# Forming every third low part of a mixer's later weights on GpSimd instead of VectorE

## The chip, the cores and the metric

The kernel runs on one core of a Trainium2 chip. The metric is the device time in microseconds, as the median of several runs. Five engines of the core matter here: PE (TensorE, the matrix products), DVE (VectorE), ACT (ScalarE), POOL (GpSimd) and SP (SyncE, which here only issues DMA transfers). Each engine works through its own instructions strictly in the order in which the program gives them, and waits on semaphores for the others.

## The reference

Two layers over 256 tokens of width 1024, all in float32. Cut to what matters:

```
for l in range(2):
    h = h + 0.5 * swiglu(rms_norm(h, ffn1_norm[l]), ffn1_w_in[l], ffn1_w_out[l])
    u = rms_norm(h, mix_norm[l])
    z_s, xbc, dt_s, qkv, z_d, b_d, a_d, gate_s, gate_d = split(u @ w_in[l])
    y_s = mamba2_branch(z_s, xbc, dt_s, ...)      # SSD in chunks of 128: decay matrices, a gated norm
    y_d = deltanet_branch(qkv, z_d, b_d, a_d, ...)  # gated delta rule in chunks of 64, a gated norm
    merged = sigmoid(gate_s) * (y_s @ ssm_w_branch[l]) + sigmoid(gate_d) * (y_d @ dn_w_branch[l])
    h = h + merged @ w_out[l]
    h = h + 0.5 * swiglu(rms_norm(h, ffn2_norm[l]), ffn2_w_in[l], ffn2_w_out[l])
return rms_norm(h, final_norm)
```

## The kernel before

All weights are streamed from DRAM once, as half units of 128 x 1024 float32. For each, SP issues a DMA into one of five buffers (`wraw`). ACT makes a copy rounded to a shorter float form (`whi`, the high part, line 68), and DVE subtracts: `wlo = wraw - whi` (the low part, line 71). PE then forms three products for each piece of weights, high by high, high by low and low by high, which together stand for a float32 product. `whi` and `wlo` have five buffers each, so parts are made some units ahead of PE, and a weight buffer comes free when its low part is done. The function `prep(i)` makes the two parts of half unit i of the list `plan`; `take()` hands PE the next one and starts loads and parts ahead.

Each layer is a feed-forward part, the mixer and a second feed-forward part. In the mixer, the string `ORDER` is the sequence of steps in the program: `z`, `k`, `q`, `v`, `b`, `d`, `x`, `g` with digits are steps that take two half units each (projections of the input), and `N` takes eight (the product of the delta branch with its output weights). Other letters are steps without weights: `s` scalars, `M` masks, `I` the triangular inverse, `R` the recurrence, `P` the products of the SSD branch with themselves, `D` the decay matrices, `S` and `T` the SSD products of one of four groups, `o` and `y` the first transposes for the two output products.

Names that the later parts use, with lines of the profile:

- `xs` (lines 340, 345, 346): PE's projection to a group's SSD input; `ca` (line 74): its short convolution, three steps on DVE per tile; `xsT`: the result, made by ACT; `xsb` (line 1101): PE's transposes of it; `xD`, `xdt`, `xe`: what DVE makes from them; `ydb`, `yob` (lines 1115, 1121): the SSD products.
- `dc` (lines 1061, 71, 78): a group's decay matrix, 128 x 2048. A DMA spreads it from DRAM (`rdram`), DVE subtracts `ac`, clamps it, ACT takes the exponential, DVE multiplies by `cbt`, PE uses it in `ydb`. It lies where `kP` or `qP` lay before, which PE reads last in `ksb` or `qsb`, the products of the recurrence.
- `cbb` (lines 1045, 1046): products of the SSD branch, in PSUM banks that the recurrence's `ob` used before; DVE's `vb<-ob,os` reads `ob` and thereby frees its bank. `cbt`: `cbb` masked by DVE.
- `so`, `srr` (line 210): inverse square roots, on POOL; `sss` and `jk` the sums of squares ahead of them; `yz`: the SSD result, scaled by `srr` on ACT.
- `oT`, `yT` (line 1154): PE's transposes for the output products; `og`, `bh`, `bl`: those results times the gate (DVE), their high part (ACT) and low part (DVE); `b` (lines 335 to 337): the delta branch's output product, whose weights are the eight half units of `N`. `o` is the last output product, of `ml` with its weights; `ob` above is another thing.

The program is written once in the sequence of `ORDER`; a scheduler then sets the order of each engine's instructions from priorities and its own costs. So an instruction that goes to another engine also shifts the others. Tiles bear numbers, which are the same before and after the change. The first layer's numbers are shown below; the second layer's mixer has the same order with other numbers.

Of the kernel before, what the change touches and what calls it, by code (L numbers as in the profile page):

```python
# [11 lines left out]
ALU = mybir.AluOpType  # L12
# [33 lines left out]
ORDER = """  # L46
z20 s z10 z11 s z21 s M k1 k0 q1 k2 k3 K1 K0 q3 q0 K3 K2 v0 q2 I Q0 I Q3 I z30 v1 z31 Q2 v2 V0 I v3
V1 I V3 I Q1 V2 d0 R R R b3 R b2 b0 R b1 R d2 R x00 R d1 x01 R d3 R R P R g100 g101 D0 S0 x10 T0 D1
x11 g110 g111 S1 x20 T1 o x21 N D2 y S2 D3 x30 x31 T2 g000 g010 g001 S3 g011 T3
""".split()  # L50


@with_exitstack
def trunk_kernel(ctx, tc, x, wst, wsm, norms, lpar, rpar, cst, out):
    nc = tc.nc
    V, A, G, PE = nc.vector, nc.scalar, nc.gpsimd, nc.tensor
# [10 lines left out]
    def act(o, i, func=AF.Copy, **kw):  # L67
        return A.activation(out=o, in_=i, func=func, **kw)  # L68

    def tt(o, a, b, op):  # L70
        return V.tensor_tensor(out=o, in0=a, in1=b, op=op)  # L71
# [9 lines left out]
    def f(ap):  # L81
        return ap.bitcast(F32)
# [15 lines left out]
    mix = (n_dram - 2 * DEPTH * (4 * FC + 22)) // DEPTH  # L98
    plan, stream = [], []

    def plan_plain(j, n):
        for i in range(j, j + n):
            stream.append(("w", i))
            plan.append(("d", [len(stream) - 1], len(stream)))
        return j + n

    def plan_ffn(j):


        o, j2, held = j + 4 * FC, j + 4 * FC + 22, []  # L110
        for kind in FFN:
            if kind in "fc":
                j = plan_plain(j, 4 if kind == "f" else 2)
            elif kind == "d":
                o = plan_plain(o, 1)
            elif kind == "A":
                y = len(stream)
                stream.extend([("y", o), ("w", o + 1), ("w", o + 2)])
                plan.append(("q0", (y, y, y + 1), y + 2))
                plan.append(("q1", (y, y + 1, y + 2), y + 3))  # L120
                plan.append(("q2", (y + 1, y, y + 2), y + 3))
                plan.append(("q3", (y, o + 3), y + 3))
                held.append((y, o + 2))
                o += 4
            else:
                y, b22 = held.pop(0)
                stream.append(("w", b22))
                plan.append(("q4", (len(stream) - 1,), len(stream)))
                stream.append(("w", b22 + 1))
                plan.append(("q5", (len(stream) - 1,), len(stream)))  # L130
                plan.append(("q6", (y,), len(stream)))
        return j2

    j0 = 0
    for _ in range(DEPTH):
        j0 = plan_ffn(plan_plain(plan_ffn(j0), mix))
    assert j0 == n_dram
    n_raw = len(stream)
    limit = []
# [15 lines left out]
    def add_to(r, i):  # L155
        G.dma_start(out=r[:], in_=tile_of(i), accum_op=ALU.add)
# [17 lines left out]
    def prep(i):  # L174
        kind, js, _ = plan[i]
        hi = wpool.tile([P, 1024], F32R, tag="whi", name="whi", bufs=NSPL)
        lo = wpool.tile([P, 1024], F32R, tag="wlo", name="wlo", bufs=NSPL)
        r = raws[js[0]]
        with ExitStack() as behind:
            for ins in state["behind"].pop(i, ()):  # L180
                behind.enter_context(tc.issue_after(ins))
            state["whi"] = act(hi[:], r[:])
            if kind in ("q1", "q2"):
                to, by = (raws[k][:] for k in js[1:])
                tt(to, to, by, ALU.add)
            if i in state["late"]:
                behind.enter_context(tc.issue_after(state["late"].pop(i).ins))
            tt(lo[:], r[:], f(hi[:]), ALU.subtract)
        if kind == "q0":
            tt(r[:], r[:], raws[js[2]][:], ALU.add)  # L190
        elif kind == "q3":
            add_to(r, js[1])
        for k in {"q0": (), "q1": (), "q2": js[::2], "q3": ()}.get(kind, (js[0],)):
            raws.pop(k)
        halves[i] = (hi, lo)
# [6 lines left out]
    def take():  # L202
        j = state["taken"]
        state["taken"] = j + 1
        ahead("loaded", limit[min(j + NSPL, n_forms) - 1], load)
        ahead("prepped", min(j + 1 if state["hold"] else j + NSPL, n_forms, state["cap"]), prep)
        return halves.pop(j)
# [82 lines left out]
    def norm_first(nw):  # L290

        place_input()
        with tc.high_priority(offset=PRI):
            _, turn0 = rms_chain(0, nw)
            ins, turn1 = rms_chain(1, nw)
            state["behind"][0], state["late"][0] = [state["square"].ins], ins
            ahead("prepped", 1, prep)
            with tc.issue_after(state["whi"].ins):
                first = turn0(0)
            with tc.issue_after(first[0].ins):  # L300
                done = turn1(0)
        for i in range(1, 4):
            state["behind"][i] = [done[0].ins]
            state["late"][i] = done[1]
        state["turns"] = {8: (turn0, 1), 11: (turn1, 1)}
        state["first_chunk"] = True

    def norm_in(nw, add):

        place_input()  # L310
        for t in range(2):
            with tc.high_priority(offset=PRI), ExitStack() as behind:
                added = add(t)
                if t == 0:
                    behind.enter_context(tc.issue_after(state["sums"][5].ins))
                ins, turn = rms_chain(t, nw)
                if t == 0:
                    turn(0)
                    done = turn(1)
            n = state["taken"]  # L320
            if t == 0:
                state["hold"] = False
                with tc.issue_after(ins.ins):
                    ahead("prepped", n + 2, prep)
                state["behind"][n + 2] = [d.ins for d in done]
            else:

                state["behind"][n + 4] = (state["square"].ins, ins.ins)
                state["late"][n + 2] = added
                state["late"][n + 3] = ins  # L330
                state["turns"] = {i: (turn, n_) for n_, i in enumerate(TURN)}
                state["cap"] = n + 4
# [954 lines left out]
    for t in range(2):  # L1287
# [4 lines left out]
        for i, (c0, c1) in enumerate(cuts):  # L1292
            junk = tmp2("junk")
            act(junk[:, : c1 - c0], h[:, t, c0:c1], AF.Square, scale=1.0 / 32.0, accum_out=ss[:, i : i + 1])
            n = c0 // 512
# [143 lines left out]
```

## Time and profile before

| What | Value |
| --- | --- |
| Median of three runs | 1544.3 us (1543.25 to 1544.58) |
| Span of the profiled execution | 1539.7 us |
| The median's part outside that span | 4.6 us |
| Weights read from DRAM over the span | 297.72 MB, 195 GB/s |
| Low parts on DVE from `wraw` | 488, 591.8 us in all |
| Busy time of POOL | 81.8 us |

The span is the time from the first to the last instruction of the one execution that the profile shows; the runs are timed from outside. Busy time of an engine that is not the bottleneck costs nothing, so the waits of PE, and the chain of work that ended last, are what to read. A row of the chain gives the start and the length in microseconds, then the engine, the tile and the line. In the timeline, instructions of one line that follow one another are put together in one row with their count, and the bracket behind a row says how long the engine stood idle and who released it. A DVE or ACT instruction's length includes about 0.08 us in which the next one has already begun; the step from one start to the next is that much shorter.

### The profile page before, as it was taken

The numbers are of one execution on the slowest core, as the hardware profiler recorded it, in microseconds if no ns is written. First come the engines' busy times: TensorE is split into PE (matmuls) and PEld (weight loads), VectorE is DVE, ScalarE is ACT, GpSimd is POOL, SyncE is SP. The second block draws the span as 40 slices with busy tenths as digits, with TensorE's granted clock in tenths as the row PEclk, the third lists the DMA queues.
The fourth block names the chain that finished last, engine by engine and source line by source line (L and its number), as shares of the span: only waits on it lengthen the run. The fifth ranks groups of instructions, "written<-read, shape, count | busy, mean of one in ns | idle before, by whom it ended". The sixth has DMA issues, their size and how long they took to land.

```text
span 1539.7 us, 29072 instructions
## 1 busy us (share of the span) xinstructions
PE 1522.8 (99%) x11473; PEld 1384.4 (90%) x11473; DVE 1229.7 (80%) x1859; ACT 944.8 (61%) x1532; POOL 81.8 (5%) x92
## 2 busy tenths in 40 slices
PE   8999999999999999999999999999999999999998
PEld 7999889999888888999899998899998888899997
DVE  6878769967899766789778887689589996677886
ACT  5655667765665645555555566676756666455565
POOL 0000110000000000000100012010000000000010
PEclk9999999999999999999999999999999999999999
DMA  7687775653565556587867687665345555556785
GB/s 277 190 265 231 226 228 167 187 164 111 178 213 171 163 166 196 185 256 211 261 225 225 208 253 229 197 193 180 117 141 202 179 170 186 176 177 195 247 241 156
DMA packets 98831, 305.73 MB, mean 199 GB/s; under 512 B 22837, under 2 KB 23813, under 8 KB 97670
## 3 DMA queue, kind: packets, MB, share of 16 engines
q1 hardware_dynamic: 93796, 290.95, 57.2%
q0 software_dynamic: 4608, 12.58, 5.1%
q8 instruction: 90, 1.47, 0.4%
q14 instruction: 47, 0.39, 0.1%
q10 hardware_dynamic: 290, 0.33, 0.1%
HBM read 297.72 MB, written 1.92 MB: 195 GB/s over the span
## 4 chain that ended last, share of the span: by engine, by line
PE 89%; DVE 4%; ACT 2%; DMA 2%; issue 1%; SPq 1%; POOL 0%; POOLq 0%; ACTq 0%; DVEq 0%
PE fc L346 10%; PE fc L340 9%; PE fc L345 9%; PE t L366 9%; PE o L337 4%; PE o L335 4%; PE o L336 4%; PE f L366 3%; PE b L335 3%; PE b L337 3%; PE b L336 3%; PE p L336 2%; PE p L337 2%; PE p L335 2%; PE xs L345 1%; PE xs L340 1%
## 5 line engine op out<-in xcount | busy, mean ns | idle before, releaser
L71 DVE TENSOR_TENSOR wlo<-wraw,whi 128x1024 fp32r<-128x1024 f32 x488 | 591.8, 1221 | 186.7 <-ACT whi L68 172.2
L68 ACT ACTIVATE whi<-wraw 128x1024 fp32r<-128x1024 f32 x488 | 511.6, 1059 | 271.0 <-PE fc L345 92.5
L346 PE MATMUL fc<-uW,wlo 128*128 128x256 f32 x1280 | 354.9, 277 | 0.0
L340 PE MATMUL fc<-uW,whi 128*128 128x256 f32 x1280 | 354.1, 277 | 0.0
L345 PE MATMUL fc<-uW,whi 128*128 128x256 f32 x1260 | 348.3, 276 | 0.0
L340 PEld LDWEIGHTS fc<-uW,whi 128*128 128x128 f32 x1280 | 240.5, 188 | 0.8
L346 PEld LDWEIGHTS fc<-uW,wlo 128*128 128x128 f32 x1280 | 240.5, 188 | 0.0
L345 PEld LDWEIGHTS fc<-uW,whi 128*128 128x128 f32 x1260 | 236.5, 188 | 0.8
L366 PE MATMUL t<-whi,uW 128*128 128x512 f32 x512 | 165.3, 397 | 0.0
L366 PEld LDWEIGHTS t<-whi,uW 128*128 128x128 f32 x512 | 95.9, 188 | 21.6 <-issue 1.3
L68 ACT ACTIVATE whi<-wsum 128x1024 fp32r<-128x1024 f32 x64 | 68.0, 1062 | 58.8 <-PE fc L345 32.9
L366 PE MATMUL t<-wlo,uW 128*128 128x512 f32 x256 | 100.2, 392 | 0.0
L71 DVE TENSOR_TENSOR wlo<-wsum,whi 128x1024 fp32r<-128x1024 f32 x64 | 78.2, 1221 | 7.9 <-ACT whi L68 5.6
L335 PE MATMUL b<-whi,bh 128*128 128x512 f32 x192 | 76.1, 398 | 0.3
L336 PE MATMUL b<-wlo,bh 128*128 128x512 f32 x192 | 74.9, 390 | 0.0
L337 PE MATMUL b<-whi,bl 128*128 128x512 f32 x192 | 74.2, 393 | 0.0
L340 PE MATMUL xs<-uW,whi 128*128 128x256 f32 x256 | 72.8, 284 | 0.0
L346 PE MATMUL xs<-uW,wlo 128*128 128x256 f32 x256 | 71.4, 279 | 0.0
L345 PE MATMUL xs<-uW,whi 128*128 128x256 f32 x254 | 70.6, 278 | 0.0
L335 PE MATMUL o<-whi,gh 128*128 128x512 f32 (+1 forms) x160 | 62.0, 388 | 0.0
L337 PE MATMUL o<-whi,gl 128*128 128x512 f32 (+1 forms) x160 | 61.8, 386 | 0.0
L336 PE MATMUL o<-wlo,gh 128*128 128x512 f32 (+1 forms) x160 | 61.7, 386 | 0.0
(337 smaller groups left out, 3291.7 us busy)
## 6 DMA issues: line engine op xcount, KB each, us to landing
wraw<-in_wst_dram SPq DMA_DIRECT2D x504, 512.0 KB, 4.9
wsum<-in_wst_dram SPq DMA_DIRECT2D x16, 512.0 KB, 7.3
wsum<-in_wst_dram POOLq DMA_DIRECT2D x16, 512.0 KB, 8.7
dc<-rdram SPq DMA_DIRECT2D x8, 1024.0 KB, 8.5
nw<-in_norms_dram SPq DMA_DIRECT2D x6, 512.0 KB, 5.9
h<-u POOLq DMA_DIRECT2D x12, 256.0 KB, 6.8
gb<-rdram SPq DMA_DIRECT2D x8, 256.0 KB, 5.6
h<-in_x_dram SPq DMA_DIRECT2D x4, 256.0 KB, 3.7
```

Source lines behind the costliest of these rows:

```text
L68: return A.activation(out=o, in_=i, func=func, **kw)
L71: return V.tensor_tensor(out=o, in0=a, in1=b, op=op)
L335: PE.matmul(ps, lh, rh, start=start, stop=False)
L336: PE.matmul(ps, lh, rl, start=False, stop=False)
L337: return PE.matmul(ps, ll, rh, start=False, stop=stop)
L340: PE.matmul(ps, wh, mh, start=start, stop=False)
L345: PE.matmul(ps, wh, ml, start=False, stop=False)
L346: PE.matmul(ps, wl, mh, start=False, stop=stop)
L366: ins = PE.matmul(ps[t][:], st, mv, start=k0 == 0 and j == 0, stop=k0 == KT - 2 and j == 5)
```

## The change

A set `SHARED` names fifteen steps of `ORDER`, 36 half units of each mixer. Those of them whose index in `plan` leaves 1 when divided by 3, twelve in each mixer and 24 in all, have their low part formed by GpSimd. The operation is the same subtraction with the same operands. The line numbers of all that follows grow by 3 to 13.

```
+SHARED = "x00 x01 d3 g100 g101 x10 x11 g110 g111 x20 x21 N x30 x31 g000".split()
...
-    j0 = 0
+    j0, third = 0, set()
     for _ in range(DEPTH):
-        j0 = plan_ffn(plan_plain(plan_ffn(j0), mix))
+        j0 = plan_ffn(j0)
+        at = len(plan) + 4
+        for name in ORDER:
+            n = 8 if name == "N" else 2 if name[0] in "zkqvbdxg" else 0
+            if name in SHARED:
+                third.update(i for i in range(at, at + n) if i % 3 == 1)
+            at += n
+        j0 = plan_ffn(plan_plain(j0, mix))
...
-            tt(lo[:], r[:], f(hi[:]), ALU.subtract)
+            if i in third:
+                G.tensor_tensor(out=lo[:], in0=r[:], in1=f(hi[:]), op=ALU.subtract)
+            else:
+                tt(lo[:], r[:], f(hi[:]), ALU.subtract)
```

Outside the mixers' second halves no engine's order changes. The twelve low parts of the first layer are `wlo_4414`, `4689`, `4757`, `4958`, `5000`, `5192`, `5272`, `5362`, `5506`, `5634`, `5687` and `5802`. Three places follow at which the order of other instructions changes.

**The place of `cbb`.** DVE before, from the last `ca` of an `xs` tile on:

```order
L74 SCALAR_TENSOR_TENSOR ca_4814<-xs_4747,lp_2175,ca_4814 128x253 [waits DVE_49]
L71 TENSOR_TENSOR wlo_4859<-wraw_4692,whi_4858 128x1024 [waits DMAHW0_49,PE_49,Activation_49]
L71 TENSOR_TENSOR wlo_4958<-wraw_4748,whi_4957 128x1024 [waits DMAHW1_49,PE_49,Activation_49]
L71 TENSOR_TENSOR dc_5029<-dc_5029,ac_2267 128x2048 [waits DMAHW5_49]
L71 TENSOR_TENSOR vb_2285<-ob_4918,os_4840 128x512 [waits PE_49]
L71 TENSOR_TENSOR cbt_4930<-cbb_4931,cs_79 128x256 [waits PE_49]
L71 TENSOR_TENSOR cbt_4930<-cbb_4936,cs_79 128x256 [waits PE_49]
```

and after:

```order
L77 SCALAR_TENSOR_TENSOR ca_4814<-xs_4747,lp_2175,ca_4814 128x253 [waits DVE_49]
L74 TENSOR_TENSOR dc_5029<-dc_5029,ac_2267 128x2048 [waits DMAHW4_49]
L74 TENSOR_TENSOR wlo_4859<-wraw_4692,whi_4858 128x1024 [waits DMAHW0_49,PE_49,Activation_49]
L81 TENSOR_SCALAR dc_5029<-dc_5029 128x2048 [waits DVE_49]
L74 TENSOR_TENSOR vb_2285<-ob_4918,os_4840 128x512 [waits PE_49]
L74 TENSOR_TENSOR cbt_4930<-cbb_4931,cs_79 128x256 [waits PE_49]
L74 TENSOR_TENSOR cbt_4930<-cbb_4936,cs_79 128x256 [waits PE_49]
L74 TENSOR_TENSOR cbt_4930<-cbb_4941,cs_79 128x256 [waits PE_49]
```

`wlo_4958` has gone to POOL, the subtraction on `dc_5029`, which waits for its transfer, has moved ahead of `wlo_4859`, and the clamp of `dc_5029` has moved ahead of `vb<-ob,os`. SP at the same place before:

```order
L171 DMA wraw_4754<-in_wst_dram 128x1024 [waits DMAHW5_49,DVE_49]
L171 DMA wraw_4850<-in_wst_dram 128x1024 [waits DMAHW6_49,DVE_49]
L171 DMA wraw_4856<-in_wst_dram 128x1024 [waits DMAHW7_49,DVE_49]
L1061 DMA dc_5029<-rdram_2271 128x2048 [waits PE_49]
L1061 DMA dc_5182<-rdram_2271 128x2048 [waits PE_49]
L171 DMA wraw_4955<-in_wst_dram 128x1024 [waits DMAHW0_49,DVE_49]
```

and after:

```order
L181 DMA wraw_4754<-in_wst_dram 128x1024 [waits DMAHW5_49,DVE_49]
L181 DMA wraw_4850<-in_wst_dram 128x1024 [waits DMAHW6_49,Pool_49]
L1074 DMA dc_5029<-rdram_2271 128x2048 [waits PE_49]
L181 DMA wraw_4856<-in_wst_dram 128x1024 [waits DMAHW7_49,DVE_49]
L1074 DMA dc_5182<-rdram_2271 128x2048 [waits PE_49]
L181 DMA wraw_4955<-in_wst_dram 128x1024 [waits DMAHW1_49,Pool_49]
```

The transfer of `dc_5029` has moved ahead of one load, `wraw_4856`, and two of these loads now wait for POOL.

**The place of the third `dc` and the `xsb` behind it.** DVE before, ahead of the last `ca` tile of the `xs` that is transposed:

```order
L71 TENSOR_TENSOR wlo_5192<-wraw_4991,whi_5191 128x1024 [waits DMAHW1_49]
L74 SCALAR_TENSOR_TENSOR ca_5123<-xs_5056,lp_2175,ca_5123 128x254 [waits DVE_49]
L71 TENSOR_TENSOR wlo_5198<-wraw_4997,whi_5197 128x1024 [waits DMAHW2_49,PE_49,Activation_49]
L74 SCALAR_TENSOR_TENSOR ca_5123<-xs_5056,lp_2175,ca_5123 128x253 [waits DVE_49]
L74 SCALAR_TENSOR_TENSOR ca_5249<-xs_5188,lp_2175,ca_5249 128x255 [waits Activation_49]
L71 TENSOR_TENSOR wlo_5266<-wraw_5057,whi_5265 128x1024 [waits DMAHW3_49,Activation_49]
L74 SCALAR_TENSOR_TENSOR ca_5249<-xs_5188,lp_2175,ca_5249 128x254 [waits DVE_49]
L71 TENSOR_TENSOR wlo_5272<-wraw_5063,whi_5271 128x1024 [waits DMAHW4_49,Activation_49]
L74 SCALAR_TENSOR_TENSOR ca_5249<-xs_5188,lp_2175,ca_5249 128x253 [waits DVE_49]
L71 TENSOR_TENSOR wlo_5302<-wraw_5189,whi_5301 128x1024 [waits DMAHW5_49,Activation_49]
L74 SCALAR_TENSOR_TENSOR ca_5255<-xs_5188,lp_2175,ca_5255 128x255 [waits Activation_49]
L71 TENSOR_TENSOR dc_5754<-dc_5754,ac_2267 128x2048 [waits DMAHW6_49]
```

and after:

```order
L74 TENSOR_TENSOR wlo_5198<-wraw_4997,whi_5197 128x1024 [waits DMAHW2_49,PE_49,Activation_49]
L74 TENSOR_TENSOR dc_5754<-dc_5754,ac_2267 128x2048 [waits DMAHW7_49]
L77 SCALAR_TENSOR_TENSOR ca_5249<-xs_5188,lp_2175,ca_5249 128x255 [waits Activation_49]
L74 TENSOR_TENSOR wlo_5266<-wraw_5057,whi_5265 128x1024 [waits DMAHW3_49,Activation_49,Pool_49]
L77 SCALAR_TENSOR_TENSOR ca_5249<-xs_5188,lp_2175,ca_5249 128x254 [waits DVE_49]
L81 TENSOR_SCALAR dc_5754<-dc_5754 128x2048
L77 SCALAR_TENSOR_TENSOR ca_5249<-xs_5188,lp_2175,ca_5249 128x253 [waits DVE_49]
L74 TENSOR_TENSOR wlo_5302<-wraw_5189,whi_5301 128x1024 [waits DMAHW5_49,Activation_49]
L74 TENSOR_TENSOR dc_5754<-dc_5754,cbt_4930 128x2048 [waits Activation_49]
L77 SCALAR_TENSOR_TENSOR ca_5255<-xs_5188,lp_2175,ca_5255 128x255 [waits Activation_49]
L77 SCALAR_TENSOR_TENSOR ca_5255<-xs_5188,lp_2175,ca_5255 128x254 [waits DVE_49]
L74 TENSOR_TENSOR wlo_5308<-wraw_5195,whi_5307 128x1024 [waits DMAHW6_49,Activation_49,Pool_49]
```

`wlo_5192` and `wlo_5272` have gone to POOL; the three steps on `dc_5754` have moved in among the low parts, ahead of the last `ca`. On SP the transfer of `dc_5754` stood one row ahead of the load of `wraw_5195`, and now stands one row behind it; that load waits for POOL, for `wlo_5192`. On PE, 14 products of the next `xs` have moved ahead of the transposes.

**The start of the delta branch's output product.** ACT before:

```order
L68 ACTIVATE jk_5475,sss_5473<-yz_2398 128x512 [waits DVE_49]
L68 ACTIVATE whi_5505<-wraw_5305 128x1024 [waits DMAHW3_49,PE_49]
L68 ACTIVATE jk_5478,sss_5473<-yz_2398 128x512 [waits DVE_49]
L68 ACTIVATE ca_5557<-xs_5496,lp_2175 128x256 [waits PE_49,Activation_49]
L68 ACTIVATE bh_5492<-og_5490 128x512 [waits DVE_49]
L68 ACTIVATE xsT_5357<-ca_5426 128x256 [waits DVE_49,Activation_49]
L68 ACTIVATE yz_2398<-yz_2398,srr_5481 128x512 [waits Pool_49]
L68 ACTIVATE yz_2398<-yz_2398,srr_5481 128x512 [waits Activation_49]
L68 ACTIVATE whi_5586<-wraw_5359 128x1024 [waits DMAHW4_49]
```

and after:

```order
L71 ACTIVATE jk_5475,sss_5473<-yz_2398 128x512 [waits DVE_49]
L71 ACTIVATE whi_5505<-wraw_5305 128x1024 [waits DMAHW3_49,PE_49]
L71 ACTIVATE xsT_5357<-ca_5426 128x256 [waits DVE_49,Activation_49]
L71 ACTIVATE jk_5478,sss_5473<-yz_2398 128x512
L71 ACTIVATE ca_5557<-xs_5496,lp_2175 128x256 [waits PE_49]
L71 ACTIVATE whi_5586<-wraw_5359 128x1024 [waits DMAHW4_49]
L71 ACTIVATE yz_2398<-yz_2398,srr_5481 128x512 [waits Pool_49]
L71 ACTIVATE yz_2398<-yz_2398,srr_5481 128x512 [waits Activation_49]
L71 ACTIVATE bh_5492<-og_5490 128x512 [waits DVE_49]
```

`bh_5492`, which PE's first `b` needs, stood ahead of the two `yz`, and now stands behind them and behind `whi_5586`. POOL before:

```order
L210 TENSOR_TENSOR so4_2294<-so_4926,mhalf_96 128x4 [waits DVE_49]
L210 TENSOR_TENSOR srr_5178<-sss_5170,mhalf_96 128x2 [waits DVE_49]
L210 TENSOR_TENSOR srr_5481<-sss_5473,mhalf_96 128x2 [waits DVE_49]
L210 TENSOR_TENSOR srr_5993<-sss_5985,mhalf_96 128x2 [waits DVE_49]
L210 TENSOR_TENSOR srr_6219<-sss_6211,mhalf_96 128x2 [waits DVE_49]
```

and after:

```order
L223 TENSOR_TENSOR srr_5178<-sss_5170,mhalf_96 128x2 [waits DVE_49]
L199 TENSOR_TENSOR wlo_5272<-wraw_5063,whi_5271 128x1024 [waits DMAHW4_49,Activation_49,Pool_49]
L199 TENSOR_TENSOR wlo_5362<-wraw_5263,whi_5361 128x1024 [waits DVE_49,PE_49,DMAHW0_49,Activation_49,Pool_49]
L199 TENSOR_TENSOR wlo_5506<-wraw_5305,whi_5505 128x1024 [waits DVE_49,PE_49,DMAHW3_49,Activation_49,Pool_49]
L223 TENSOR_TENSOR srr_5481<-sss_5473,mhalf_96 128x2 [waits DVE_49]
L199 TENSOR_TENSOR wlo_5634<-wraw_5497,whi_5633 128x1024 [waits DMAHW6_49,Activation_49,Pool_49]
```

`srr_5481`, which the two `yz` wait for, now has `wlo_5506` ahead of it, whose high part is `whi_5505` above. On PE, ten transposes `oT` stood between the last `xs` product and the first `b`; now twelve and four `yT` stand there.

## The prediction

> **What bounds the kernel now.** I read the page first: busy shares, the chain that ended last, the costliest groups.
>
> ```profile
> span 1539.7 us, 29072 instructions
> PE 1522.8 (99%) x11473; PEld 1384.4 (90%) x11473; DVE 1229.7 (80%) x1859; ACT 944.8 (61%) x1532; POOL 81.8 (5%) x92
> PE 89%; DVE 4%; ACT 2%; DMA 2%; issue 1%; SPq 1%; POOL 0%; POOLq 0%; ACTq 0%; DVEq 0%
> L71 DVE TENSOR_TENSOR wlo<-wraw,whi 128x1024 fp32r<-128x1024 f32 x488 | 591.8, 1221 | 186.7 <-ACT whi L68 172.2
> ```
>
> PE is busy 99% of the span, so all that a change off PE can win is the time in which PE stands still. A low part costs DVE 1.22 us; 24 of 488 leave it. The windows of the first layer's mixer show where DVE is short.
>
> ```profile
> 390.00:440.00 50.00, 49.40 (x386) 43.83 (x385) 45.48 (x62) 32.51 (x50) 2.61 (x2) 1.00 0.61 201
> 410.00:420.00 10.00, 10.00 (x66) 9.00 (x65) 10.00 (x9) 8.50 (x8) 0.00 (x0) 1.00 0.34 88
> 440.00:450.00 10.00, 9.07 (x97) 8.48 (x97) 10.00 (x12) 5.08 (x7) 0.00 (x0) 1.00 0.64 209
> ```
>
> The columns after the length are PE, PEld, DVE, ACT and POOL. DVE is saturated at 410 and 440 and POOL idle, yet PE loses only 0.60 us in the first 50 and 0.93 in 440 to 450. PE's waits by name in the second mixer (us in total, times, longest); the first has the same rows for `xsb` and `o`, and the last line for `cbb`:
>
> ```profile
> PE cbb L1045 <- DVE vb L71: 1.3, 1, 1.3
> PE xsb L1101 <- ACT xsT L68: 0.9, 1, 0.9
> PE o L337 <- DVE ml L71: 0.3, 1, 0.3
> ...
> PE cbb L1045 <- DVE vb L71: 0.6, 1, 0.6
> ```
>
> The largest conceivable gain is therefore about 2.5 + 1.8 = 4.3 us over both layers. Against it stands what the new order and the slower engine put in.
>
> **The price of one low part on POOL.** No row has it. These are the nearest:
>
> ```profile
> L249 POOL MEMSET Y<- 128x512 f32 x2 | 1.0, 524 | 0.3 <-POOLq L1428 0.3
> L726 POOL MEMSET Q<- 128x2048 f32 x2 | 3.6, 1808 | 0.0
> L819 POOL TENSOR_TENSOR c<-c,pq 128x4 f32<-128x4 f32 x8 | 1.6, 200 | 0.6
> 458.66 1.61 POOL L210 TENSOR_TENSOR srr<-sss,mhalf 128x2 f32<-128x2 f32 x1 [25.77 <-DVE sss L79]
> 527.29 0.70 POOL L210 TENSOR_TENSOR srr<-sss,mhalf 128x2 f32<-128x2 f32 x1 [18.70 <-DVE sss L79]
> 458.49 1.22 DVE L71 TENSOR_TENSOR wlo<-wraw,whi 128x1024 fp32r<-128x1024 f32 x1
> ```
>
> The fills give (1808 - 524) / 1536 = 0.84 ns a column, so one stream of 1024 is 0.86 us. Lower bound: one stream and the small operation's 0.20, 1.06 us. Upper: two reads and a write one after another, 0.20 + 3 x 0.86 = 2.8 us. I take 2.2, nearer the upper end because the operation reads two operands, which the fills don't. [...]
>
> The same `srr` takes 0.70 us at 527 and 1.61 at 458, where DVE's `wlo` is running beside it and ends at 459.71; POOL ends 0.56 later. So POOL can be held up by such a DVE instruction; whether POOL holds up DVE is open.
>
> **Part 1, removed from DVE:** 12 x 1.22 = 14.6 us a layer, worth nothing by itself where PE doesn't wait. ACT's high parts, DMA count and PE's products are unchanged. The low parts themselves are mostly early enough. The tightest is the second of three here:
>
> ```profile
> 470.87 4.85 ACT L68 ACTIVATE whi<-wraw 128x1024 fp32r<-128x1024 f32 x5
> 472.25 3.49 DVE L71 TENSOR_TENSOR wlo<-wraw,whi 128x1024 fp32r<-128x1024 f32 x3
> 476.59 0.39 PE L336 MATMUL b<-wlo,bh 128*128 128x512 f32 x1
> ```
>
> Its high part ends near 472.9 (two of five at 0.97), POOL would end at 475.1 and PE needs it at 476.6: cost 0, cover 1.5 us. If it is gone, PE waits for POOL by what is over.
>
> **Part 2, the `cbb` place.** DVE now takes `dc<-dc,ac`, which waits for a transfer, ahead of a low part, and a clamp of `dc` ahead of `vb`, whose bank PE waits for; SP issues that transfer one weight load earlier.
>
> ```profile
> 392.37 1.24 DVE wlo L71
> 393.62 0.33 SPq L171
> 394.00 7.91 DMA dc<-rdram
> 401.94 2.29 DVE dc L71
> 404.23 0.61 DVE vb L71
> 404.88 0.70 PE cbb L1045 x2
> L954 PE MATMUL ksb<-St,kP x16: 272/273/323, 391.3 to 392.1; 128*64 128x128 f32 x16
> L78 DVE TENSOR_SCALAR dc<-dc x2: 1218/1219/1220, 408.3 to 412.8; 128x2048 f32<-128x2048 f32 x2
> ```
>
> Before, SP's load waits for the low part that ends at 393.6 and `dc` goes at 394.0. Now it can go once PE has read the old tile (last at 392.1, ending near 392.4): up to 1.6 earlier. Behind its landing DVE has a low part and a clamp more, 2 x 1.14 = 2.3 us from start to start. Net +0.7 to +2.3, straight onto PE, which already waits there; +1.2 taken, nearer the early issue because no other row holds SP back. Queued behind the waiting `dc` on DVE are the low part, `vb` and the masks.
>
> **Part 3, the `xsb` place.** Ahead of the last `ca` DVE loses two low parts (-2.3) and gains a clamp and a `dc` product (1.14 + 2.20); PE comes later to the transposes by 14 `xs` products that moved ahead of them.
>
> ```profile
> 443.56 0.49 DVE ca L74
> 444.12 0.42 ACT xsT L68
> 444.59 0.44 PE xsb L1101 x2
> 445.03 0.12 PE xs L346
> 431.12 1.22 DVE L71 TENSOR_TENSOR wlo<-wraw,whi 128x1024 fp32r<-128x1024 f32 x1
> DMA to landing us min/median/max: 8.5/8.9/9.3
> L1061 SPq DMA_DIRECT2D dc<-rdram x3: 371/425/1490, 394.0 to 424.2; - x3
> ```
>
> That is +1.1 on DVE against 14 x 0.12 = 1.6 on PE: -0.5. But the third `dc` is now wanted seven rows earlier, where DVE began low parts at 431.1 and 432, and SP issues it behind a weight load that waits for a low part on POOL. Issued at 424.2 and landed 8.5 later it was there at 432.7; one or two us later it holds DVE, with the `ca` rows behind it that PE's transposes need, and the later weight loads on SP, for as long. -0.9 (the whole wait gone) to +3; I take +0.5, a wait of 1.0.
>
> **Part 4, the start of the delta branch.** This is the largest term. PE's first `b` needs `bh`. On ACT `bh` was ahead of the two `yz`; now it stands behind them, and `yz` waits for POOL's `srr`, which stands behind a low part.
>
> ```profile
> 456.70 1.06 ACT L68 ACTIVATE whi<-wraw 128x1024 fp32r<-128x1024 f32 x1 [0.21 <-PE xs L345]
> 458.76 0.62 ACT L68 ACTIVATE bh<-og 128x512 fp32r<-128x512 f32 x1
> 460.30 1.34 ACT L68 ACTIVATE yz<-yz,srr 128x512 f32<-128x512 f32 x2 [0.61 <-POOL srr L210]
> 458.04 1.25 PE L1154 MATMUL oT<-cs,vb 128*128 128x128 f32 x10
> 459.44 0.50 PE L335 MATMUL b<-whi,bh 128*128 128x512 f32 x1
> ```
>
> Count from the high part's start, 456.7. PE reached `oT` at 458.04 and had 10 transposes (1.1) before `b` at 459.44, a stall of 0.3. Now 16 transposes (0.11 each, 1.8) stand there, so PE is ready at 3.2 behind the high part. The chain becomes high part 1.06, low part on POOL 2.2, `srr` 0.70, two `yz` 1.25 from start to start, `bh` 0.63, and 0.2 for hand-overs: 6.0. PE waits 2.8 where it waited 0.3: +2.5. If POOL cost nothing, ACT's own row (high part, `xsT`, `jk`, `ca`, a second high part, `yz`, `bh`) still ends near 5.4: +1.9. If `srr` is held by DVE as in the 1.61 row, and the low part takes 2.8 and is held too, +5. I take +2.5.
>
> **Sum.** 1.2 + 0.5 + 2.5 = 4.2 a layer, 8.4 for two: span 1539.7 to 1548.1. The runs' median is 1544.3, 4.6 us over the profiled span; with the same on top, 1552.7, say 1553. Summed lower ends (0.7 - 0.9 + 1.9) x 2 = +3; upper (2.3 + 3 + 5) x 2 = +21. 0.2%, 3.1 us, is about what a measurement of this kernel can tell from no change.
>
> **Rivals.**
> - Nothing to measure, 1543 to 1547. DVE, 14.6 us lighter, is ahead everywhere: `dc` early and the POOL parts hidden, so parts 2 and 3 give back both stalls, and only part 4's floor of 1.9 x 2 is left: 1544.3 - 4.3 + 3.8 = 1543.8. For it: DVE at 10.00 of 10. Against: in part 2 what is late is the transfer, not DVE's load.
> - Faster, 1540. The place is part 4: if PE arrives at `b` over 2.5 us later than I count, ACT's chain is hidden, and the two stalls of DVE go: 1544.3 - 4.3 = 1540. It decides at a PE lateness of 2.5; against it, the order puts only 6 more transposes there.
> - DVE is held by POOL. DVE's two-input instructions stand still while a low part is read. Each of 12 then takes up to 2.2 from DVE where it gave back 1.22; DVE's spare time is 50 - 45.48 = 4.5 us in the first window. 12 x (2.2 - 1.22) = 11.8, less 4.5: up to 7 a layer on PE, beside part 4: 1544.3 + 14 + 5 = 1563. It decides once DVE loses over 1.2 + 4.5 / 12 = 1.6 us to each low part on POOL. For it: the 1.61 row shows the conflict from POOL's side. Against: no row shows DVE's. [...]
>
> **How the numbers follow.** The order on the engines is fixed by the program, so parts 2 and 4 are likeliest: 0.57 for the forecast (own range 1548 to 1559). Held DVE 0.18 (1557 to 1566). No measurable change 0.17. Faster 0.08. Slower is then 0.75. The range leaves out faster and the worst of the held case: 1545 to 1563.
>
> **What would show it.** Low parts on POOL of 2.0 to 2.8 us; DVE busy down by 24 x 1.22 = 29 us; PE waiting for `bh` from ACT for 2 to 3 us in each layer, for `cbb` on `vb` longer than 0.6 and 1.3. Wrong, if the first `b` waits under 1 us, if DVE's `wlo` near POOL's take far over 1.22, or if PE waits for `wlo` itself.

## The result, and the profile after

| | before | after |
| --- | --- | --- |
| Median of the runs | 1544.16 us | 1567.58 us (1566.81 to 1569.47, four runs) |
| Ratio, with its 95% interval | | 1.016 (1.0147 to 1.0172) |
| Span of the profiled execution | 1539.7 us | 1565.0 us |
| Mean granted TensorE clock over the span | 0.999 | 0.992 |

The change costs 23.4 us. The direction of the forecast was right and its size was not: 8.4 us had been summed, and the time lies above the range.

The page of the profile after, its span, busy times and the two kinds of low part (columns of a group: count, busy us, mean ns, idle time before):

```profile
span 1565.0 us, 29077 instructions
PE 1532.4 (98%) x11473; PEld 1393.0 (89%) x11473; DVE 1221.8 (78%) x1835; ACT 944.1 (60%) x1532; POOL 146.7 (9%) x116
L74 DVE TENSOR_TENSOR wlo<-wraw,whi 128x1024 fp32r<-128x1024 f32 x464 | 572.8, 1242 | 195.2 <-ACT whi L71 178.8
L199 POOL TENSOR_TENSOR wlo<-wraw,whi 128x1024 fp32r<-128x1024 f32 x24 | 62.6, 2607 | 161.0 <-ACT whi L71 95.8
```

24 low parts left DVE, which is 24 x 1.22 = 29.3 us; DVE's busy time fell from 1229.7 to 1221.8, by 7.9. So 21.4 us came back, 0.9 us for each low part that POOL makes. PE, with the same instructions, is busy 9.6 us longer. The windows that the prediction read:

```profile
390.00:440.00 50.00, 46.59 (x370) 41.60 (x369) 39.82 (x51) 29.46 (x45) 14.35 (x7) 0.97 0.59 194
410.00:420.00 10.00, 10.00 (x38) 8.06 (x37) 8.95 (x9) 4.18 (x9) 2.99 (x1) 0.83 0.15 34
440.00:450.00 10.00, 7.50 (x37) 6.05 (x35) 9.54 (x8) 6.89 (x7) 2.65 (x1) 1.00 0.40 134
```

PE's waits in the second mixer (us in total, times, longest; the first differs in `xsb` alone, 2.6):

```profile
PE cbb L1058 <- DVE vb L74: 3.4, 1, 3.4
PE b L348 <- ACT bh L71: 3.2, 1, 3.2
PE xsb L1114 <- ACT xsT L71: 2.3, 1, 2.3
```

PE waits at exactly the three places that the prediction named. Over both mixers these waits come to 18.1 us, against 3.7 before (0.6 + 1.3 at `cbb`, 0.9 twice at `xsb`): 14.4 us more. The rest is in the windows, in the column behind POOL's, the granted clock. In the window from 410 PE is busy for all of 10 us and gets 38 products done, at a clock of 0.83. In steps of 2 us, behind the wait at `cbb` and behind the one at `b` (length, PE busy and count, granted clock, DMA share, GB/s):

```profile
410.00:412.00 2.00, 2.00 (x6) 0.50 0.00 0
412.00:414.00 2.00, 2.00 (x7) 0.65 0.00 0
472.00:474.00 2.00, 2.00 (x6) 0.50 0.09 35
474.00:476.00 2.00, 2.00 (x9) 0.79 0.19 25
```

PE runs at half rate for about 3.4 us. (1 - 0.50) x 2 + (1 - 0.65) x 2 = 1.7 us are lost in the first two rows. Summed so over 2 us windows, the first mixer loses 5.1 us and the second 6.9; the trace before loses none in its mixers. 14.4 + 12.0 = 26.4 us, against 25.3 between the two spans. The 12.0 is an upper figure, since PE stands still in part of one of these stretches; its busy time grew by 9.6.

**The place of `cbb`**, SP, POOL and DVE in the timeline after (start, length, engine, row; in brackets idle time and releaser):

```profile
394.27 0.33 SPq L181 DMA_DIRECT2D wraw<-in_wst_dram  x1
394.65 0.48 SPq L1074 DMA_DIRECT2D dc<-rdram  x1
401.06 2.37 POOL L199 TENSOR_TENSOR wlo<-wraw,whi 128x1024 fp32r<-128x1024 f32 x1 [6.82 <-ACT whi L71]
401.51 4.07 DVE L74 TENSOR_TENSOR dc<-dc,ac 128x2048 f32<-128x2048 f32 x1 [1.98 <-DMA dc<-rdram]
405.50 1.21 DVE L74 TENSOR_TENSOR wlo<-wraw,whi 128x1024 fp32r<-128x1024 f32 x1
406.64 1.21 DVE L81 TENSOR_SCALAR dc<-dc 128x2048 f32<-128x2048 f32 x1
407.77 0.68 DVE L74 TENSOR_TENSOR vb<-ob,os 128x512 f32<-128x512 f32 x1
```

`dc` took 2.29 us before and takes 4.07 where a low part runs on POOL: the difference, 1.78, is close to what of POOL's instruction was left when DVE's began (403.43 - 401.51 = 1.92). The second mixer has the same rows with another overlap:

```profile
1173.77 2.36 POOL L199 TENSOR_TENSOR wlo<-wraw,whi 128x1024 fp32r<-128x1024 f32 x1 [6.83 <-ACT whi L71]
1175.69 2.58 DVE L74 TENSOR_TENSOR dc<-dc,ac 128x2048 f32<-128x2048 f32 x1 [3.46 <-DMA dc<-rdram]
```

Here 0.44 us of POOL's low part were left, and `dc` takes 0.29 longer. So the hold is most of the added wait in the first mixer and little of it in the second.

And the transfer was hardly issued earlier. It can go once `ksb` has read the old tile. Before, it went 2.7 us behind the start of `ksb` (391.29 to 394.00); now it goes 2.55 us behind (392.10 to 394.65), because SP's weight load ahead of it waits for a low part that POOL began at 391.88 and made in 2.37 us (394.25), and goes at 394.27. Behind `dc` on DVE stand a low part and the clamp, then `vb`, as the order had shown.

**The place of `xsb`**, DVE and ACT after:

```profile
439.16 2.29 DVE L74 TENSOR_TENSOR dc<-dc,ac 128x2048 f32<-128x2048 f32 x1 [2.22 <-DMA dc<-rdram]
441.77 3.04 DVE L74 TENSOR_TENSOR wlo<-wraw,whi 128x1024 fp32r<-128x1024 f32 x1
446.37 1.91 ACT L71 ACTIVATE dc<-dc 128x2048 f32<-128x2048 f32 x1 [2.75 <-DVE dc L81]
448.30 1.28 ACT L71 ACT_TABLE_LOAD   x1
449.59 0.42 ACT L71 ACTIVATE xsT<-ca 128x256 f32<-128x256 f32 x1
```

DVE idles 2.2 us for the third `dc`, then a low part on DVE itself takes 3.04. ACT, in its own order, must take the exponential of that `dc` and a table load before `xsT`, which PE waits for; before the change the exponential stood behind this `xsT` (451.78 against 444.12).

**The start of `b`**, the four engines after, and ahead of them the same small DVE instruction at a place where POOL rests:

```profile
434.77 0.17 DVE L82 TENSOR_SCALAR sss<-sss 128x2 f32<-128x2 f32 x1
465.12 1.06 ACT L71 ACTIVATE whi<-wraw 128x1024 fp32r<-128x1024 f32 x1 [1.34 <-PE xs L358]
466.32 2.44 POOL L199 TENSOR_TENSOR wlo<-wraw,whi 128x1024 fp32r<-128x1024 f32 x1 [10.46 <-ACT whi L71]
467.13 1.65 DVE L82 TENSOR_SCALAR sss<-sss 128x2 f32<-128x2 f32 x1
468.86 0.70 POOL L223 TENSOR_TENSOR srr<-sss,mhalf 128x2 f32<-128x2 f32 x1
469.59 1.34 ACT L71 ACTIVATE yz<-yz,srr 128x512 f32<-128x512 f32 x2 [1.09 <-POOL srr L223]
470.83 0.61 ACT L71 ACTIVATE bh<-og 128x512 fp32r<-128x512 f32 x1
471.50 0.80 PE L348 MATMUL b<-whi,bh 128*128 128x512 f32 x1 [3.20 <-ACT bh L71]
```

This is the chain that the prediction wrote out: 6.38 us from the high part's start to `b`, where it had 6.0. Even an instruction of 128 x 2 on DVE, `sss`, stands still until POOL ends: 1.65 us against 0.17. POOL ends at 468.76, `sss` at 468.78.

### The profile page after: what moved, and what is told of

It is laid out like the page before. It is cut to its first block, busy times and chain, and to the rows that moved or that the text cites. A ratio compares the mean times of both kernels' runs of the same rounds, so it can differ in the third digit from the quotient of the medians.

```text
span 1565.0 us, 29077 instructions
## 1 busy us (share of the span) xinstructions
PE 1532.4 (98%) x11473; PEld 1393.0 (89%) x11473; DVE 1221.8 (78%) x1835; ACT 944.1 (60%) x1532; POOL 146.7 (9%) x116
## 3 DMA queue, kind: packets, MB, share of 16 engines
HBM read 297.72 MB, written 1.92 MB: 191 GB/s over the span
## 5 line engine op out<-in xcount | busy, mean ns | idle before, releaser
L74 DVE TENSOR_TENSOR wlo<-wraw,whi 128x1024 fp32r<-128x1024 f32 x464 | 572.8, 1242 | 195.2 <-ACT whi L71 178.8
L74 DVE TENSOR_TENSOR wlo<-wsum,whi 128x1024 fp32r<-128x1024 f32 x64 | 78.2, 1222 | 7.5 <-ACT whi L71 5.6
L199 POOL TENSOR_TENSOR wlo<-wraw,whi 128x1024 fp32r<-128x1024 f32 x24 | 62.6, 2607 | 161.0 <-ACT whi L71 95.8
```

Source lines behind the costliest of these rows:

```text
L199: G.tensor_tensor(out=lo[:], in0=r[:], in1=f(hi[:]), op=ALU.subtract)
```

## The experiments

Two theories stood at the start. A: the order is to blame, three waits of PE that the scheduler put in, with the clock that falls behind them. B: POOL's reading is to blame, since it holds up DVE and delays whatever waits for POOL. Diffs are against the kernel after where its name is given, else against the kernel before. All times stand against runs of the kernel before on the same chip.

**One place mended: `bh` ahead of the two `yz` again** (kernel after).

```
-                act(yv, yv, scale=rr[:, t : t + 1])
+                behind.enter_context(tc.issue_after(state["bh"].ins))   # for g == 1
+                act(yv, yv, scale=rr[:, t : t + 1])
```

> The changed kernel with one order mended: ACT's first bh is issued ahead of the two yz of the second group, in both layers; POOL's twelve low parts a mixer, and the cbb and xsb places, stay as they are. Theory (three stalls of PE a mixer, set by order and lengthened by POOL's hold on DVE, each followed by some 3.4 us at half clock): the stall of 3.4 us ahead of the first b falls to about 1, the clock behind it stays at 1.00, so 2 x (2.4 + 1.7) = 8 us go: about 1559. Rival 1 (the low clock has a cause of its own and stays): 1563. Rival 2 (the late low part on POOL, not ACT's order, sets the first b): 1567, nothing gained.

Measured: 1562.46 us (1558.8 to 1566.0), ratio 1.0121 (1.0105 to 1.0137). PE's waits for `b` in the second mixer:

```profile
PE b L350 <- DVE bl L74: 1.2, 1, 1.2
PE b L348 <- ACT bh L71: 0.7, 1, 0.7
```

The wait for `bh` is down to 0.7, but `bl` behind it is late by 1.2, so 5.1 us came back of the 8 expected, and the median is near rival 1. In the trace no low clock is left behind `b` in either mixer. The four runs tell of the clock: spans of 1557.0, 1559.9, 1561.5 and 1564.2 us go with mean clocks of 0.997, 0.994, 0.992 and 0.992. In the profiled execution, the one at 1557.0, the first mixer has waits of 3.4 at `cbb` and at `xsb` and loses nothing to the clock behind either; the second loses 3.4.

**The same place alone, in the kernel before: `bh` behind the two `yz`.** All low parts stay on DVE.

```
+                if hp == 0:
+                    behind.enter_context(tc.issue_after(state["scaled", 1].ins))
                 act(oh[:].rearrange("p a t -> p (a t)"), og[:])
```

> The kernel before, all low parts on DVE and POOL as it was, with one order of the change put in: ACT's first bh is issued behind the two yz of the second group, in both layers; up to there the order is that of before. Theory (this order alone delays the first b): PE's wait ahead of the first b rises from 0.3 to about 2, with perhaps a low clock behind it: 1547 to 1551. Rival (only together with POOL's low part ahead of srr): 1543 to 1545.

Measured: 1548.21 us, ratio 1.0032 (1.002 to 1.0043). PE's wait for `b`, the same in both mixers:

```profile
PE b L335 <- ACT bh L68: 2.4, 1, 2.4
```

Order alone makes PE wait 2.4 us here, in each layer, and the time is in the theory's range. The prediction's floor of part 4 was 1.9 over a wait of 0.3, that is 2.2.

**The `cbb` place mended: DVE's first subtraction on `dc` behind `vb`** (kernel after). The scheduler then also moves the third `dc` and puts `bh` back.

```
+                if g == 0:
+                    behind.enter_context(tc.issue_after(state["vb"].ins))
                 tt(dc[:], dc[:], ac[...], ALU.subtract)
```

> The changed kernel, all 24 low parts on POOL, with one order pinned: DVE's first subtraction on dc is issued behind vb<-ob,os. The scheduler then also puts bh ahead of yz again and the third dc behind more of the ca steps, so the order at all three places is near that of before. Theory (order makes the stalls): all three stalls under 1.5 us, no low clock, 1543 to 1548. Rival (POOL's slower low parts and its hold on DVE make the loss, whatever the order): 1557 or more.

Measured: 1554.97 us, ratio 1.0072 (1.0059 to 1.0085). PE's longest waits in both mixers:

```profile
PE t L379 <- DVE sss L82: 2.9, 1, 2.9
PE xsb L1117 <- ACT xsT L71: 1.7, 1, 1.7
```

Half of the loss is gone with the wait at `cbb`, and other waits are in its place; the time lies between the theory's range and the rival's. In the timeline of this kernel POOL and DVE hold each other:

```profile
481.39 7.74 POOL L199 TENSOR_TENSOR wlo<-wraw,whi 128x1024 fp32r<-128x1024 f32 x2 [3.58 <-ACT whi L71]
483.46 6.76 DVE L74 TENSOR_TENSOR wlo<-wraw,whi 128x1024 fp32r<-128x1024 f32 x2
```

Two low parts on POOL take 7.74 us and two on DVE beside them 6.76, where alone they take 2 x 2.37 and 2.36. What this kernel still loses has both causes in it, so order and reading had to be tested apart.

**Order without POOL's reading** (kernel after). POOL fills the 24 low parts with zeros instead of subtracting.

```
-                G.tensor_tensor(out=lo[:], in0=r[:], in1=f(hi[:]), op=ALU.subtract)
+                with tc.issue_after(state["whi"].ins):
+                    G.memset(f(lo[:]), 0.0)
...
+                if g == 1:
+                    behind.enter_context(tc.issue_after(state["vb"].ins))   # second dc
```

> The changed kernel's order on DVE, ACT, SP and PE but for a few neighbouring rows, without POOL's reading: in place of each of the 24 subtractions POOL fills the low part with zeros (the low parts of these 24 half units are left out of the computation), which reads nothing; DVE is relieved as in the change, and the second dc is pinned behind vb, as it was. Theory (the order makes part of the stalls, POOL's reading, which holds DVE, the rest): DVE's instructions beside POOL's have their old lengths, the stall at cbb is near 2 us instead of 3.5, at xsb near 1 instead of 2.6, ahead of the first b near 2 instead of 3.4, and few low clocks follow: 1549 to 1557. Rival 1 (POOL's hold is all of it): 1540 to 1545. Rival 2 (the order is all of it): 1564 or more.

Measured: 1550.33 us, ratio 1.0049 (1.0037 to 1.0062). Its page, and POOL's group:

```profile
PE 1528.3 (99%) x11473; PEld 1389.4 (90%) x11473; DVE 1205.2 (78%) x1835; ACT 946.1 (61%) x1532; POOL 107.5 (7%) x116
L200 POOL MEMSET wlo<- 128x1024 f32 x24 | 23.5, 979 | 158.0 <-PE xs L360 64.2 <-PE b L350 47.8 <-PE t L380 25.7
```

The `dc` at the place of `cbb` in its timeline:

```profile
401.79 2.29 DVE L74 TENSOR_TENSOR dc<-dc,ac 128x2048 f32<-128x2048 f32 x1 [2.50 <-DMA dc<-rdram]
```

PE's longest waits in its first mixer:

```profile
PE ob L1009 <- ACT vn L71: 2.1, 1, 2.1
PE b L349 <- ACT bh L71: 2.0, 1, 2.0
```

DVE's busy time is 1205.2, close to the 1200.4 that the count of instructions gives, and `dc` takes 2.29 (POOL's fill beside it ends 0.14 us after it began). The transfer of `dc` is now issued 1.2 us behind the start of `ksb` (393.30 to 394.46), as early as the prediction had taken it, because the load ahead of it no longer waits for a low part on POOL. DVE still idles 2.5 us for it, since the order puts `dc` ahead of other work. PE waits 0.2 us at `xsb`, with the exponential of `dc` still ahead of `xsT` on ACT: that wait needs POOL's reading. Ahead of the first `b` 2.0 us remain.

So about 7 of the 23.4 us are there without any reading by POOL; some 16 come with it. Two limits belong to this. A fill takes 0.98 us where the subtraction takes 2.61, so the 16 hold both POOL's longer instruction, for which loads and `srr` wait, and its hold on DVE. And the order differs in a few rows: here `dc` stands ahead of the last `ca`, so that ACT's `xsT` and `vn` wait with it, and PE's wait has moved from `cbb` ahead to `ob`. The split is good to a few microseconds.

**POOL's reading without the order.** DVE, ACT and SP keep the order of the kernel before and make all low parts; POOL reads SBUF beside the same 24 units, into a tile that nobody uses.

```
+            if i in third:
+                for c in range(4):
+                    G.tensor_tensor(out=spare[:], in0=cs[:, c*224:(c+1)*224], in1=f(hi[:, c*224:(c+1)*224]), op=ALU.subtract)
```

> The kernel before, with all low parts on DVE and the order of DVE, ACT and SP exactly as before; added is work on POOL alone: beside each of the same 24 half units, once its high part is there, four subtractions of 224 columns each, reading a constant and the high part and writing a spare tile that nobody reads. Theory (POOL's reading holds DVE, but it is the order that puts this on PE's path): some DVE instructions near them take 0.5 to 2 us more, the span grows by 2 to 6 us: 1546 to 1550. Rival 1 (order alone): 1544, no DVE instruction longer. Rival 2 (contention alone makes the loss): 1560 or more.

Measured: 1561.33 us, ratio 1.0111 (1.0097 to 1.0125). POOL's group on the page:

```profile
L200 POOL TENSOR_TENSOR spare<-cs,whi 128x224 f32<-128x224 f32 x96 | 111.5, 1162 | 125.8 <-ACT whi L70 119.8
```

PE's longest waits in its first mixer:

```profile
PE xsb L1114 <- ACT xsT L70: 2.3, 1, 2.3
PE b L348 <- ACT bh L70: 2.2, 2, 2.0
```

POOL ahead of the first `b`:

```profile
461.96 4.56 POOL L200 TENSOR_TENSOR spare<-cs,whi 128x224 f32<-128x224 f32 x4 [10.38 <-ACT whi L70]
466.48 0.70 POOL L222 TENSOR_TENSOR srr<-sss,mhalf 128x2 f32<-128x2 f32 x1
```

With no instruction moved on another engine, this work on POOL costs 17 us, above the theory's range and inside rival 2's: work beside DVE cost PE time here without any change of order. It is not a measure of the change's own reading: POOL's rows take 111.5 us here against 62.6 for the 24 low parts, and DVE keeps its low parts. Nor is all of it DVE standing still: its busy time rose by 9.5 us, to 1239.2. At `b` it is POOL's queue: `srr` stands behind these rows and ends at 467.18, though `sss`, which it needs, was there by 462.77, and the two `yz` and the second `bh` follow. The shares are not separated. Some 3 of the 16.8 us by which this trace is longer lie, by PE's progress, where POOL has no added row, and are not explained. That 7 and 17 add up to 24 is no proof of a sum.

**The clock: PE kept busy in the three waits** with products that nobody uses (kernel after).

```
+                for _ in range(FILL_C if g == 2 else 0):        # 5 at cbb; 22 transposes at xsb, 8 products at b
+                    PE.matmul(cbb[:], ident, cs[:, 0:512], start=True, stop=True)
```

> The changed kernel with matrix products that nobody reads laid into PE's three waits of each mixer: five plain float32 products of 512 columns ahead of the third cbb, 22 repeats of one transposition at xsb, eight products of 512 columns ahead of the first b (about 2.6, 2.4 and 4.2 us of PE). No work is taken away, the wait for the data is as long as before. Theory (PE's standing still is what lowers the clock): the granted clock stays near 1.00 behind all three places, 6 x 1.7 = 10 us go, less what the products overrun: 1557 to 1561. Rival (the clock falls for another reason, or the clock is only a symptom): 1567 or more, with 0.5 in the windows behind the places as now.

Measured: 1582.21 us, ratio 1.0245 (1.023 to 1.0261), with mean clocks of 0.997 and 0.998 in all four runs against 0.990 to 0.993. The clock stayed at 1.00 behind five of the six places. At `xsb` in the first mixer two waits of 1.8 us were left, and 6.8 us at half rate follow; the same two waits in the second mixer (1.9 each) have none behind them. The products outlasted the waits (those at `cbb` took 4.5 us and those at `b` 7.0 in the first mixer, where 2.6 and 4.2 were meant), and PE's busy time rose by 23 us to 1555.5, so the gain in time that was expected didn't come. It shows that the low clock goes with PE's idleness; it doesn't give its price.

**Four low parts in all, where DVE has time to spare** (kernel after, `SHARED` cut).

```
-SHARED = "x00 x01 d3 g100 g101 x10 x11 g110 g111 x20 x21 N x30 x31 g000".split()
+SHARED = "x30 x31 g000".split()
```

> The change for the last steps alone (x30 x31 g000): two low parts a mixer on POOL, where DVE has idle time; up to there the order is that of before. Theory (POOL's low parts cost only where DVE's work is awaited by PE): 1542 to 1546. Rival (each low part on POOL costs PE about the same, 23.4 / 24 = 1 us): 1548.

Measured: 1544.61 us in ten runs, ratio 1.0007 (0.9998 to 1.0017). POOL and DVE in its timeline:

```profile
477.64 6.26 POOL L199 TENSOR_TENSOR wlo<-wraw,whi 128x1024 fp32r<-128x1024 f32 x1 [15.50 <-DVE wlo L74]
486.64 3.42 DVE L74 TENSOR_TENSOR wlo<-wraw,whi 128x1024 fp32r<-128x1024 f32 x1
```

The hold is as strong as ever, 6.26 us on POOL and 3.42 on DVE, and it costs nothing measurable: no wait of PE in the mixers is over 1.3 us, as before.

**A better version of the kernel before, twice.** If waits of PE decide, taking away those at `cbb` and `xsb` should beat it. The first try has `vb` ahead of `dc`, and the two `yz` behind `bh`; the second has `vb` ahead of `dc`, and the first `yT` behind the first `b`.

```
+                if g == 0:
+                    behind.enter_context(tc.issue_after(state["vb"].ins))     # both: ahead of dc's subtraction
...
+                    behind.enter_context(tc.issue_after(state["bh"].ins))     # first: ahead of yz
...
+                    behind.enter_context(tc.issue_after(state["b"].ins))      # second: ahead of yT
```

> The kernel before, all low parts on DVE, with two pins: DVE's first subtraction on dc behind vb<-ob,os, and the two yz of the second group behind the first bh. Meant as a better version: PE's wait at cbb (0.9 and 1.5 us) should go. Theory (each wait of PE is set by one order on DVE or ACT): 1541 to 1543 if the other places stay as they are. Rival (the scheduler's other shifts, the third dc ahead of low parts, give it back): 1545 or more.

> The kernel before, all low parts on DVE, with two things pinned: DVE's first subtraction on dc behind vb<-ob,os (which PE's cbb waits for), and PE's first yT transposes behind the first b. It is meant to take away PE's stall at cbb (0.6 and 1.3 us before) without putting another in its place, as the last such attempt did at yT. If the stalls are all that is lost: cbb's 1.9 us go, no place of over 1.5 us is new, 1541 to 1544 us. Rival: bh stands behind a high part and a sum of squares on ACT in this order too, so PE waits 1 to 3 us for it at b, the clock may fall behind that, and the time is 1545 to 1550 us; then no reordering by pins is left that beats the kernel before.

Measured: 1549.41 us, ratio 1.0034 (1.0021 to 1.0048), and 1555.01 us, ratio 1.0076 (1.0062 to 1.0089). In both the waits at `cbb` and `xsb` are gone or under 0.3 us, and in both a longer one stands around the start of `b`. The first version's wait in its first mixer:

```profile
PE yT L1179 <- DVE og L74: 2.9, 1, 2.9
```

The second version's, and then its windows behind that wait:

```profile
PE b L335 <- ACT bh L68: 4.8, 1, 4.8
```

```profile
466.00:468.00 2.00, 2.00 (x6) 0.50 0.64 227
468.00:470.00 2.00, 2.00 (x6) 0.50 0.10 31
470.00:472.00 2.00, 2.00 (x7) 0.65 0.73 244
```

The theories failed. The first time lies in its rival's range, the second above its rival's. In the second version the scheduler put `bh` behind two high parts and both `yz`, and one wait of 4.8 us a layer, with 3.4 us lost to the clock behind each, makes a kernel that moves no low part 12 us slower. No version here beat the kernel before.

## Why the prediction was right or wrong, point by point

**The step that failed** is the sum: three waits were added up to 8.4 us, as if nothing followed from a wait, and as if DVE's rows kept their lengths. By the terms of the sum the waits grew by some 14 us (part 2 by 4.9 over both layers, part 3 by 3.1, part 4 by 5.8, where 2.4, 1.0 and 5.0 were taken), and 9.6 to 12 us of low clock, which had no term, came behind them.

**The bound and the ceiling** were right: PE alone decides, low parts came early enough, and PE never waited for a `wlo` of POOL's. These have a mean of 2.61 us, where 2.2 was taken and 2.8 was the upper bound; alone they take 2.36 to 2.40, beside busy DVE up to 3.5. Of the 4.3 us to be won nothing was won.

**Part 4** was right in mechanism and in size: +2.5 taken, +2.9 measured (a wait of 3.2 against a stall of 0.3), and the kernel before with this one change of order shows 2.4 by itself. POOL's own part of it is then 0.8.

**Part 2** had the path right and two terms wrong. It took 2.3 us for the two rows behind the landing of `dc`, which they cost, and 1.1 us off for an earlier issue, "because no other row holds SP back". One did: the weight load ahead of it, which waits for POOL. The order rows ahead of the prediction showed that load's semaphore change to POOL's, and the sum left it out. Counted from PE's own arrival at this place (404.28 before, 405.14 after in the first mixer), `dc` was issued only 0.2 us earlier in either mixer. In the first its transfer then took 6.9 us instead of 7.9, which no row explains, and landed 1.3 us earlier after all. What the sum lacked there was a longer `dc`, whose length it held fixed: -1.3 + 2.3 + 1.8 = +2.8. In the second mixer the landing gained 0.5 and the hold is 0.3: -0.5 + 2.3 + 0.3 = +2.1. 1.2 was taken and 2.3 was the upper end.

**Part 3** was mis-sized: +0.5 taken, +1.7 and +1.4 measured. Its chain ended at DVE's last `ca` (the row of 2.20 that it calls a product is the subtraction on `dc`, of the same length). The chain that PE waits for runs on through ACT's exponential and table load, 1.91 + 1.28 us: `xsT` begins 2.9 us behind the last `ca` (446.73 to 449.59), where it was 0.1 before. The danger that it named, the late transfer (2.2 us idle on DVE), and a held low part of 3.04 on DVE lie ahead in the same chain; without POOL's reading PE waits 0.2 here.

**The clock** was missing altogether, and is the largest error: 9.6 to 12 us of 25. Ahead of the run, the trace before showed no wait of PE over 1.3 us in the mixers, and no low clock there, so it had no row for it; but the same trace has the clock at 0.50 from 1535.7 us to its end, behind 3.4 us in which PE was busy for 1.14, and a prediction that puts waits of 2.8 us in has to ask for it. In the mixers of the eleven traces here the clock fell to 0.50, for 3.4 us or twice that, and the length of a wait alone does not tell whether: waits of 2.0 to 2.3 us were sometimes enough, and one of 3.4 us sometimes was not:

| Kernel | PE's waits over 1.5 us, first and second mixer | lost to the clock |
| --- | --- | --- |
| before | none; none | 0; 0 |
| after | 3.4, 3.2, 2.6; 3.4, 3.2, 2.3 | 5.1; 6.9 |
| `bh` ahead again | 3.4, 3.4; 3.4, 2.6 | 0; 3.4 |
| `vb` ahead of `dc` | 2.9, 1.7; 2.9, 1.7 | 1.7; 1.7 |
| order without reading | 2.1, 2.0; 2.3, 2.0 | 3.4; 1.7 |
| reading without the order | 2.3, 2.0; 2.3, 1.6 | 1.7; 0 |
| PE kept busy | 1.8, 1.8; 1.9, 1.9 | 3.4; 0 |
| four low parts | none; none | 0; 0 |
| before, `bh` behind `yz` | 2.4, 1.7; 2.4 | 0; 1.7 |
| before, first better version | 2.9; 2.9 | 1.7; 1.7 |
| before, second better version | 4.8; 4.8 | 3.4; 3.4 |

The losses come in steps of 1.7 us, one for each 3.4 us at half rate. The traces also show which waits brought a step. In the kernel after, the clock falls in the mixers at 410.00, 450.96, 471.44, 1181.41, 1222.37 and 1242.85 us; all distances between these are whole multiples of 3.413 us (12, 18, 226, 238 and 244 of them from the first). So in this trace the clock changed on one grid of 3.413 us through 833 us, and what counted was how a wait lay on it. With each trace cut into stretches of 3.413 us on its own grid, 19 of the 20 falls in all mixers stand behind a stretch in which PE was busy for at most 1.49 us, and every such stretch there is followed by one. Of the stretches with 1.51 us or more one is, in the kernel with added products (1.66). In the kernel "order without reading", a wait of 2.1 us lies whole in the stretch from 402.36, which leaves 1.31 us busy, and the clock falls at 405.77. In "`bh` ahead again", the wait of 3.4 us at `cbb` is cut by the grid: PE is busy 1.84 us in the stretch from 401.98 and 1.62 in the next, and the clock stays. A second step followed in the four cases in which PE was still busy for no more than 2.4 us of the first stretch at half rate. Where the grid lies differed between traces (counted from the span's start, its first edge is at 0.4 us in the kernel after, 2.6 in "`bh` ahead again", 3.0 in "order without reading"), so by this the same program would get another number of steps in another run; there is one trace of each kernel, so that is not shown.

**The rival "DVE is held by POOL"** was a right mechanism and wrongly set apart. It was priced as an alternative to the forecast, at 0.18, while nothing made the two exclude each other: order and hold are both in this change, and each makes the other's waits longer. Its point of decision was 1.6 us lost on DVE per low part. The mean over all is 0.9, below it, and it decided nevertheless, together with POOL's longer instruction (16 of 23 us go where POOL only fills): the hold did not spread over DVE's spare time, it fell on `dc`, on `wlo` and on `sss` just where PE's next input hung on them. The rows show the hold where POOL read: `dc` took 4.07 us instead of 2.29, and `sss`, which has one input tile, 1.65 instead of 0.17, so it was not two-input instructions alone. Where POOL filled, DVE's subtractions did not show it: a low part on DVE that begins at 489.71, 0.07 us into a fill of 0.95, takes 1.22, and the 464 low parts have a mean of 1222 ns against 1221 before. A clamp of `dc` did: beside a fill one took 1.67 us instead of 1.22 (second mixer, at 1183.86), and the mean of the eight is 1276 ns against 1220.

**Rivals "nothing" and "faster"** fell with the first list of waits: no stall of DVE's was given back.

**The range** ended at 1563: in the upper ends of the sum the hold had been added to part 4 alone, the worst of the held case was left out, and the clock was in no case.

## What to carry to other kernels

Moving element-wise work from a busy DVE to POOL was no free help here, where both read SBUF: each low part took 1.22 us off DVE and gave 0.9 back, at moments that the critical chain picked, and what waited for POOL came later (`srr` started 2.54 us behind the start of the low part ahead of it). In a kernel whose PE is 99% busy, list for each engine what the scheduler moves, and which loads and small instructions then wait for POOL. Give the sum a term for the clock: behind waits of PE of 1.8 to 3.4 us these traces lost 0, 1.7 or 3.4 us to it, and behind the two of 4.8 us 3.4 each. Work for a slower engine belongs where no one waits for either engine, as the four low parts showed, which cost nothing that could be measured (1544.61 us, ratio 1.0007).

## What the runs showed of the hardware that was not expected

- PE's granted clock fell to half 20 times in the mixers of these traces, for 3.4 or 6.8 us, on a grid of 3.413 us in each trace; 19 of the 20 stand behind a stretch of the grid in which PE was busy for at most 1.49 us. A wait of 2.0 us was enough (order without reading, ahead of `b`), and one of 3.4 us that the grid cut in two was not (`bh` ahead again, at `cbb`). Spans of one program from 1557.0 to 1564.2 us went with mean clocks from 0.997 to 0.992.
- POOL was held for longer than one instruction of DVE's: its low part of 6.26 us (kernel with four low parts) began at 477.64, while DVE worked without a pause on SBUF operands until 481.53, and ended 2.37 us, its own length, after that.
- A DVE instruction of 128 x 2 waited for the end of POOL's low part too: `sss` took 1.65 us against 0.17 and ended at 468.78, POOL at 468.76.
- A fill of 128 x 1024 on POOL took 0.98 us in the mean and didn't lengthen DVE's subtractions (1.22 beside it), though it did a clamp (1.67 against 1.22); a subtraction of the same size that reads took 2.37 us alone.
